# One task per weight split, and a seventh weight buffer in the feed forward of a two-layer decoder trunk

## The chip, the cores and the metric

The kernel runs on one NeuronCore of a Trainium2 chip. The metric is device time in microseconds, from the first to the last instruction with what the launch adds on the device. Before the change the median of three runs is 748.7 us (748.66 to 749.61).

## The reference

Two layers over 256 tokens of 1024 channels; each has a mixing part (dilated attention beside an mLSTM, with gates) and a feed forward. All of it is float32. The change concerns how the weights of all matmuls are brought in, and above all the feed forward:

```python
def hybrid_layer(x, ...):                      # DEPTH = 2
    h = rms_norm(x, norm_mix_w)
    z = h @ w_in + b_in                        # 1024 x 5640, columns go to q, k, v, gates ...
...
    yb = sigmoid(z[..., COL_MO:COL_MI]) * hm   # the mLSTM's output gate
    mixed = sigmoid(ga) * (ya @ w_proj_att) + sigmoid(gb) * (yb @ w_proj_mlstm)
    x = x + mixed @ w_out                      # 1024 x 1024
    h2 = rms_norm(x, norm_mlp_w)
    x = x + square(relu(h2 @ w_ff1)) @ w_ff2   # 1024 x 4096, 4096 x 1024
```

## The kernel before

**Weights.** Every matmul with weights is computed from float32r halves: a weight block w of 512 KB is split into hi, its rounded copy, and lo = w - hi, and TensorE multiplies hi by the activations' high and low part and lo by the high part. A *step* (class `Step`, line 237) is one such block with the 6 to 24 matmuls that use it. For each step SP loads the block into one of `N_RAW` = 6 buffers raw (line 385), ScalarE writes hi (`high`, one ACTIVATE), VectorE writes lo (`low`, one TENSOR_TENSOR), each into one of `N_SPLIT` = 5 buffers. Steps run on TensorE in the order of the list `steps`. A load waits until the block in its buffer has been split (`loads`, line 460); hi of step i waits for its block and for step i - 5 to be done (`highs`, line 495); lo waits for hi (`lows`, line 502). `highs` and `lows` are two tasks that go through all steps in order.

**Order.** Nothing in the program is ordered by hand. A scheduler (class `Scheduler`, line 299) runs at build time: tasks are generators that yield operations or flags that they need, a planner (`Plan`) keeps an estimated time for each engine and buffer, and the operation that can start soonest is written next into its engine's program; among those that start within about 0.1 us of it the lower rank wins. A split has rank 0.5 when TensorE needs it within 5 us by the plan, otherwise 4 (`slack`, line 472). On the chip each engine then runs its program strictly in order and waits on semaphores.

**Feed forward.** `w_ff1` makes eight hidden blocks of 512 channels. Blocks 0 to 5 (`BY_SEVEN`) are multiplied by `w_ff2` with seven products instead of eight (`by_seven`, line 1154); here they are called groups 0 to 5. A group has seven steps in this order: b11, t1, t3, b22, t2, b21, t4. Four have a weight load (b11, t3, b22, b21); t3's buffer first receives a block called b12. `weight_sums` (line 1138) builds the others: VectorE adds b11 + b12 into a total (t1; the totals are the tiles va and num in turn), a transfer issued by POOL then adds b22 to b12 in place (t3), another adds b22 to the total when lo of t1 is done (t2), and when lo of t2 is done VectorE adds b21 to the total (t4). So one total serves three steps, one after the other, and the buffers of b11 and b21 are only free when t1 and t4 are made. Between the groups' steps stand the `w_ff1` steps of the later hidden blocks, each block in two halves of two pieces; the first half of block 7 is called h7 below. At the end of a layer the order is: h7 (two pieces), group 4's t2, b21, t4, the second half of block 7 (two pieces), group 5's b11, t1, t3, b22, then two `w_ff2` steps of block 6, group 5's t2, b21, two more steps of block 6, group 5's t4, and four steps of block 7. The low half of a group's activations goes through a tile called zc for group after group, so that the next group's cast into zc waits until TensorE is done with t4.

**The gate's memory.** mog (line 395) has the shape of a raw buffer. It holds the mLSTM's output gate: `mog_evac` (line 808) fills it, `gates`, `output_gate` and `mlstm_out` (line 915) use it, and nothing touches it in the feed forward. The flags mix0 to mix3 are set when the four parts of `mixed` are there, at the end of the mixing part.

In the profile all operations have the line of a helper, L203, so rows are told apart by their tiles.

Of the kernel before, what the change touches and what calls it, by code (L numbers as in the profile page):

```python
# [298 lines left out]
class Scheduler:  # L299
# [8 lines left out]
    def add(self, gen, rank=3):  # L308
        self.tasks.append(Task(gen, rank))

    def mark(self, *flags):
        self.done.update(flags)
# [44 lines left out]
def trunk(ctx: ExitStack, tc: tile.TileContext, x_in, positions, norm_mix_w, w_in, b_in, conv_w, conv_b,  # L357
# [85 lines left out]


    steps, loaded = [], []
    at = {"step": 0, "part": 0.0}
    begins_at = [0.0]

    def new_step(src, view, dur, fn, raw=None, free=None):

        i = len(steps)
        load = len(loaded) if src is not None else None
        step = Step(i, raws[load % N_RAW] if raw is None else raw, load, src, view, dur, fn, free)
        if load is not None:
            loaded.append(step)
        steps.append(step)
        begins_at.append(begins_at[-1] + dur)
        return step

    def loads(first):  # L460
        for n in range(first, len(loaded)):
            yield Need(*loaded[n - N_RAW].free)
            yield load(n)
            mark(loaded[n].flag)

# [3 lines left out]
            return sync.dma_start(out=out, in_=src)  # L469
        return sync.dma_start(out=out[:, j, c], in_=src[:, j, c])  # L470

    def slack(i):

        def rank():
            k = i if isinstance(i, int) else at[i]
            now_at = begins_at[at["step"]] + at["part"] * steps[at["step"]].dur
            due = now["pe"] + begins_at[k] - now_at
            return 0.5 if due - now["act" if i == "hi" else "vec"] < 5.0 else 4
        return rank

    def high(i, j=slice(0, 2), c=slice(0, None)):
        st = steps[i]
# [9 lines left out]
            h, l, r = h[:, j, c], l[:, j, c], r[:, j, c]  # L492
        return vec.tensor_tensor(l, r, h, op=OP.subtract)

    def highs(first):
        for i in range(first, len(steps)):
            at["hi"] = i
            yield Need(("raw", i), ("step", i - N_SPLIT))
            yield high(i)
            mark(("hi", i))  # L500

    def lows(first):
        for i in range(first, len(steps)):
            at["lo"] = i
            yield Need(("hi", i))
            yield low(i)
            mark(("lo", i))


    KEEP = 2  # L510
# [248 lines left out]
    def layer(l, X, Y):  # L759
# [332 lines left out]
        def hid(f):  # L1092

            return tuple(s[:, 4 * (f % 2):4 * (f % 2) + 4, :] for s in X)
# [59 lines left out]
        def by_seven(f):  # L1154

            i = {}
            seven[f] = i
            last = f == BY_SEVEN[-1]

            def one(name, product, n, src=None, raw=None):  # L1160
                def fn(k, hi, lo):
                    yield Need(tag(f"q{f}"))
                    if product not in prods:
                        prods[product], = yield Take(banks)
                    o, new = prods[product], f == BY_SEVEN[0]
                    yield Need(("hi", k))
                    order = [(j, part) for j in range(2) for part in range(2)] + [(j, 2) for j in range(2)]
                    for at_, (j, part) in enumerate(order):
                        at["part"] = at_ / 6
                        if part == 2:  # L1170
                            yield Need(("lo", k))
                        yield mm(o[:], (shared.q_l, shared.q_h, shared.q_h)[part][:, n, j, :], (hi, hi, lo)[part][:, j, :],
                                 new and at_ == 0, last and at_ == 5 and product not in ("p2", "p3", "p4"))
                    if name == "t4":
                        mark(tag(f"seven{f}"))
                    if name == "t2" and last:
                        add(flush(), 1.5)
                step = new_step(src, wide(512), 1.395, fn, raw)
                i[name] = step.i
                return step  # L1180

            def w(kp, c):
                return rows(w_ff2[l], 4 * f + 2 * kp, 512 * c, 512)

            def total():
                return shared.total[f % 2]


            todo = (("b11", "P1", 0, w(0, 0), None), ("t1", "p5", 3, None, total), ("t3", "P7", 6, w(0, 1), None),
                    ("b22", "p3", 5, w(1, 1), None), ("t2", "P6", 4, None, total), ("b21", "p2", 1, w(1, 0), None),  # L1190
                    ("t4", "p4", 2, None, total))
            at_begin, made = len(steps) - 6, {}
            starts.append((at_begin, lambda: add(weight_sums(f, i, made), weight_rank)))

            def weight_rank():
                return slack(i["t1"])()

            for k, what in enumerate(todo):
                made[what[0]] = one(*what)
                if k in (1, 3, 5, 6):  # L1200

                    if k == 6:
                        made["b11"].free = [("lo", i["b11"]), ("raw", i["t1"])]
                        made["b21"].free = [("lo", i["b21"]), ("raw", i["t4"])]
                    if k == 3:
                        i["b12"] = ("b12", l, f)
                        made["t3"].flag = ("raw", i["b12"])
                    yield
# [160 lines left out]
        for c in range(2):  # L1369
            by_token(w_out[l], 512 * c, 512, X, (0, 1, 2, 3), out_evac(c), flags=lambda kp: [tag(f"mix{kp}")])  # L1370
        starts.append((len(steps), lambda: add(last_loads(), 3)))
        f0, f1 = {}, {}
        for kp in range(4):
            by_feature(w_ff1[l], 0, Y, (kp,), 0, 3, f0, ff_evac(0), flags=lambda kp: [tag(f"h{kp}")])
# [31 lines left out]
        if l + 1 < DEPTH:  # L1406
            for c in range(2):
                whole(7, c)
        else:
            by_token_last(w_ff2[l], lambda: hid(7), [out_norm(c) for c in range(2)], acc, 28, lambda kp: [tag(f"f7{kp}")])  # L1410

    starts = []
    X, Y = slot
# [75 lines left out]
    def first_split(n):  # L1489
        i, j, c, flags = pieces[n]  # L1490
        yield Need(f"piece{n}", ("xh", 0, 0), *[("hi", *p[:1], *f) for p in pieces[:n] for f in p[3]])
        yield high(i, j, c)
        mark(*[("hi", i, *f) for f in flags])
        yield low(i, j, c)
        mark(*[("lo", i, *f) for f in flags])
        if n + 1 == len(pieces):
            mark(("hi", 0), ("lo", 0), ("hi", 1), ("lo", 1))
            add(highs(2), slack("hi"))
            add(lows(2), slack("lo"))

    def first_x():
        yield from warm(WARM[0])
# [31 lines left out]
    def main():  # L1534
        begins = {}
        for i, fn in starts:
            begins.setdefault(i, []).append(fn)
        for i, st in enumerate(steps):
            if i in begins:
                for fn in begins[i]:  # L1540
                    fn()
            at["step"], at["part"] = i, 0.0
            yield from st.fn(i, st.view(his[i % N_SPLIT]), st.view(los[i % N_SPLIT]))
            mark(("step", i))

    at["hi"] = at["lo"] = 0
    mark(*[(kind, -i) for kind in ("step", "lo") for i in range(1, 10)])
    add(first_loads(), 0)
    add(first_params(), 2)
    add(first_constants(), 0)  # L1550
# [34 lines left out]
```

## Time and profile before

| | |
|---|---|
| median of three runs | 748.7 us (748.66 to 749.61) |
| the profiled execution | 749.45 us, of which its span is 747.6 |
| TensorE (PE) | busy 735.1 us, 98%; 5123 matmuls |
| weight loads on TensorE (PEld) | busy 674.9 us, 90% |
| VectorE (DVE) / ScalarE (ACT) / GpSimd (POOL) | busy 587.5 / 454.6 / 82.8 us |
| granted TensorE clock | 0.997 of full speed |
| DMA | 148.77 MB, mean 199 GB/s |

The span runs from the first to the last instruction. Matmuls overlap: each begins before the row of the one before it ends, so TensorE's pace is read from starts. Waits are put down to the semaphore that came last. SP's loads are issued by its queue (SPq); POOL's rows of DMA_DIRECT2D are the making of a transfer's descriptors, and its landing comes later.

### The profile page before, as it was taken

To read this page: it belongs to the slowest core of one execution; us is meant where nothing else is said; L and a number is where in the kernel's file an instruction comes from. 1 tells how busy PE (TensorE), PEld (TensorE's weight loads), DVE (VectorE), ACT (ScalarE), POOL (GpSimd) and SP (SyncE) were. 2 spreads that over 40 slices of the span, in tenths; PEclk is the share of its full clock that TensorE was granted. 3 is DMA by queue.
4 is the path that set the end of the run, shared out by engine and by line. 5 is a ranking of instruction groups with operands and counts; after the bars stand their busy time and mean duration, and the time that the engine had idled before them with its cause. 6 is when DMAs were issued, how large, how long until landed. Compare 5 with 4: busy or idle time off the path is not lost.

```text
span 747.6 us, 13242 instructions
## 1 busy us (share of the span) xinstructions
PE 735.1 (98%) x5123; PEld 674.9 (90%) x5123; DVE 587.5 (79%) x870; ACT 454.6 (61%) x708; POOL 82.8 (11%) x130
## 2 busy tenths in 40 slices
PE   9999999999999999999999999999999999999995
PEld 8989889998899999978899898899989999999774
DVE  5897887568658888977979988956776779887966
ACT  6657776545656577655656467845455756675752
POOL 4764010000010011100000000000000001101100
PEclk9999999999999999999999999999999999999998
DMA  9857553555567888877664654355555788888652
GB/s 310 294 183 222 169 164 120 191 187 181 171 196 224 239 238 235 246 198 226 234 217 130 212 179 146 115 172 194 174 190 173 181 250 216 260 253 233 190 165 85
DMA packets 90079, 148.77 MB, mean 199 GB/s; under 512 B 5176, under 2 KB 31712, under 8 KB 90016
## 3 DMA queue, kind: packets, MB, share of 16 engines
q1 hardware_dynamic: 82272, 133.63, 54.1%
q0 software_dynamic: 7440, 14.00, 10.7%
q8 instruction: 40, 0.66, 0.3%
q10 hardware_dynamic: 304, 0.30, 0.1%
q14 instruction: 23, 0.19, 0.1%
HBM read 146.32 MB, written 1.05 MB: 197 GB/s over the span
## 4 chain that ended last, share of the span: by engine, by line
PE 89%; issue 3%; DVE 3%; DMA 3%; ACT 1%; POOLq 0%; DVEq 0%; POOL 0%; ACTq 0%
PE bank L203 89%; DVE lo L203 2%; DMA raw<-in_w_ff 2%; DMA num<-in_w_ff 1%; ACT hi L203 1%; DVE x L203 0%; DVE big L203 0%; ACT slot0h L203 0%; DVE num L203 0%; DVE va L203 0%; DVE sg L203 0%; POOLq L1581 0%; POOL small L203 0%; DVEq L1581 0%; DVE small L203 0%
## 5 line engine op out<-in xcount | busy, mean ns | idle before, releaser
L203 DVE TENSOR_TENSOR lo<-raw,hi 128x1024 fp32r<-128x1024 f32 (+3 forms) x251 | 300.7, 1210 | 92.8 <-ACT hi L203 92.1
L203 ACT ACTIVATE hi<-raw 128x1024 fp32r<-128x1024 f32 (+3 forms) x251 | 259.6, 1045 | 147.4 <-PE bank L203 122.0
L203 PE MATMUL bank<-slot1l,hi 128*128 128x256 f32 x576 | 162.7, 283 | 0.0
L203 PE MATMUL bank<-slot1h,lo 128*128 128x256 f32 x576 | 162.3, 282 | 0.2 <-DVE lo L203 0.2
L203 PE MATMUL bank<-slot1h,hi 128*128 128x256 f32 x576 | 162.3, 282 | 0.0
L203 PE MATMUL bank<-slot0h,hi 128*128 128x256 f32 x576 | 161.5, 282 | 0.1
L203 PE MATMUL bank<-slot0h,lo 128*128 128x256 f32 x576 | 160.8, 283 | 0.3 <-DVE lo L203 0.3
L203 PE MATMUL bank<-slot0l,hi 128*128 128x256 f32 x576 | 160.9, 282 | 0.0
L203 PEld LDWEIGHTS bank<-slot0h,hi 128*128 128x128 f32 x576 | 107.9, 188 | 1.7 <-ACT hi L203 0.7
L203 PEld LDWEIGHTS bank<-slot1h,hi 128*128 128x128 f32 x576 | 108.3, 188 | 1.1 <-issue 0.5
L203 PEld LDWEIGHTS bank<-slot1l,hi 128*128 128x128 f32 x576 | 108.2, 188 | 1.2 <-issue 0.3
L203 PEld LDWEIGHTS bank<-slot1h,lo 128*128 128x128 f32 x576 | 108.4, 188 | 0.6 <-DVE lo L203 0.4
L203 PEld LDWEIGHTS bank<-slot0h,lo 128*128 128x128 f32 x576 | 107.5, 188 | 1.3 <-DVE lo L203 0.8
L203 PEld LDWEIGHTS bank<-slot0l,hi 128*128 128x128 f32 x576 | 107.8, 188 | 0.8 <-issue 0.2
L203 PE MATMUL bank<-hi,sg 128*128 128x512 f32 x168 | 66.5, 396 | 2.7 <-ACT hi L203 2.7
L203 PE MATMUL bank<-hi,zc 128*128 128x512 f32 x168 | 66.2, 394 | 0.0
L203 POOL DMA_DIRECT2D raw<-in_w_ff x12 | 14.5, 1210 | 365.0 <-DVE va L203 164.9
L203 PE MATMUL bank<-lo,zc 128*128 128x512 f32 x168 | 53.0, 396 | 0.2
L203 PE MATMUL bank<-hi,slot1h 128*128 128x512 f32 (+2 forms) x132 | 48.0, 364 | 0.0
L203 PE MATMUL bank<-lo,slot1h 128*128 128x512 f32 (+2 forms) x132 | 47.7, 361 | 0.0
L203 PE MATMUL bank<-hi,slot1l 128*128 128x512 f32 (+2 forms) x132 | 47.6, 361 | 0.0
L203 PE MATMUL bank<-hi,slot0h 128*128 128x512 f32 (+1 forms) x128 | 47.2, 369 | 0.0
(186 smaller groups left out, 1058.1 us busy)
## 6 DMA issues: line engine op xcount, KB each, us to landing
raw<-in_w_ff SPq DMA_DIRECT2D x128, 512.0 KB
raw<-in_w_in SPq DMA_DIRECT2D x78, 512.0 KB
raw<-in_w_out SPq DMA_DIRECT2D x16, 512.0 KB
raw<-in_w_ff POOLq DMA_DIRECT2D x12, 512.0 KB, 5.8
raw<-in_w_in SPq DMA_DIRECT2D x8, 520.0 KB
raw<-in_w_proj_mlstm SPq DMA_DIRECT2D x8, 512.0 KB
raw<-in_w_proj_att SPq DMA_DIRECT2D x8, 512.0 KB
va<-in_w_ff POOLq DMA_DIRECT2D x6, 512.0 KB, 7.7
```

The costliest lines, as they stand in the source:

```text
L203: f(*args, **kw)
```

## The change

Three things. Buffers come from a list, `ring`: a step with a load takes the buffer at its head, keeps the function that tells what frees it, and puts the buffer back at the end. Before the first feed-forward step of a layer mog is put at the head of the list, to be free when mix0 to mix3 are set, and after the last one it is taken out, so that the feed forward has seven buffers and the rest of the layer six. And `highs` and `lows` are gone: `split(i)` makes one task for each step, added when step i - 5 is done; it waits for its block alone, so a step whose block comes late no longer holds up the splits of the steps behind it in the plan.

```diff
+    ring = [(t, lambda: []) for t in raws]
...
-        step = Step(i, raws[load % N_RAW] if raw is None else raw, load, src, view, dur, fn, free)
         if load is not None:
+            raw, before = ring.pop(0)
+        step = Step(i, raw, load, src, view, dur, fn, free)
+        if load is not None:
+            step.before = before
+            ring.append((raw, lambda: step.free))
             loaded.append(step)
...
     def loads(first):
         for n in range(first, len(loaded)):
-            yield Need(*loaded[n - N_RAW].free)
+            yield Need(*loaded[n].before())
             yield load(n)
             mark(loaded[n].flag)
...
-    def highs(first):
-        for i in range(first, len(steps)):
-            at["hi"] = i
-            yield Need(("raw", i), ("step", i - N_SPLIT))
+    def split(i):
+
+        engine = ["act"]
+
+        def rank():
+            return slack(i, engine[0])
+
+        def parts_of():
+            yield Need(("raw", i))
             yield high(i)
             mark(("hi", i))
-
-    def lows(first):
-        for i in range(first, len(steps)):
-            at["lo"] = i
-            yield Need(("hi", i))
+            engine[0] = "vec"
             yield low(i)
             mark(("lo", i))
+
+        add(parts_of(), rank)
...
         starts.append((len(steps), lambda: add(last_loads(), 3)))
+
+        ring.insert(0, (mog, lambda: [tag(f"mix{k}") for k in range(4)]))
         f0, f1 = {}, {}
...
             by_token_last(w_ff2[l], lambda: hid(7), [out_norm(c) for c in range(2)], acc, 28, lambda kp: [tag(f"f7{kp}")])
+        ring[:] = [(t, free) for t, free in ring if t is not mog]
...
             mark(("step", i))
+            if i + N_SPLIT < len(steps):
+                split(i + N_SPLIT)
```

The change moves instructions at the end of each feed forward. On VectorE around group 4's t2 and t4 in layer 0, before (lo and hi are the split's buffers, raw the weight buffers, va and num the totals of groups 4 and 5, big an evacuated piece of block 7, slot0 the hidden activations):

```order
L203 TENSOR_TENSOR lo_106<-va_2045,hi_101 128x2x512
L203 TENSOR_TENSOR lo_107<-raw_96,hi_102 128x2x512
L203 TENSOR_TENSOR lo_108<-raw_97,hi_103 128x2x512
L203 TENSOR_TENSOR lo_104<-raw_98,hi_99 128x1024
L203 CAST slot0h<-big_75 128x512
L203 TENSOR_TENSOR lo_105<-raw_93,hi_100 128x1024
L203 TENSOR_TENSOR slot0l<-big_75,slot0h 128x512
L203 TENSOR_TENSOR num_2046<-raw_97,raw_98 128x1024
L203 TENSOR_TENSOR lo_106<-va_2045,hi_101 128x2x512
L203 TENSOR_TENSOR lo_107<-raw_94,hi_102 128x2x512
L203 TENSOR_TENSOR va_2045<-va_2045,raw_94 128x1024
L203 CAST slot0h<-big_76 128x512
```

and now:

```order
L203 TENSOR_TENSOR lo_106<-va_2042,hi_101 128x2x512
L203 TENSOR_TENSOR lo_108<-raw_96,hi_103 128x2x512
L203 TENSOR_TENSOR lo_107<-raw_95,hi_102 128x2x512
L203 TENSOR_TENSOR lo_104<-raw_97,hi_99 128x1024
L203 CAST slot0h<-big_75 128x512
L203 TENSOR_TENSOR lo_105<-raw_98,hi_100 128x1024
L203 TENSOR_TENSOR slot0l<-big_75,slot0h 128x512
L203 TENSOR_TENSOR lo_107<-mog,hi_102 128x2x512
L203 TENSOR_TENSOR num_2043<-raw_95,raw_96 128x1024
L203 TENSOR_TENSOR lo_106<-va_2042,hi_101 128x2x512
L203 TENSOR_TENSOR va_2042<-va_2042,mog 128x1024
L203 TENSOR_TENSOR lo_104<-raw_93,hi_99 128x1024
```

The first row is lo of t1 of group 4, followed by t3's and b22's (now b22's, then t3's), those of h7's two pieces, the sum into num for group 5, lo of t2 and the sum for t4 into va. The lo of b21 (from raw_94 before, from mog now) has moved ahead of the sum into num, and the cast of big_76 behind t4.

On SP, the loads from group 4's b22 on, with what each waits for (DVE is VectorE, Activation ScalarE, DMAHW and DMASW transfers), before:

```order
L203 DMA raw_97<-in_w_ff 128x2x512 [waits DMAHW2_49,DVE_49]
L203 DMA raw_98<-in_w_ff 128x4x256 [waits DMAHW3_49,DVE_49]
L203 DMA raw_93<-in_w_ff 128x4x256 [waits DMAHW4_49,DVE_49]
L203 DMA raw_94<-in_w_ff 128x2x512 [waits DMAHW5_49,DVE_49]
L203 DMA raw_95<-in_w_ff 128x4x256 [waits DMAHW6_49,DVE_49]
L203 DMA raw_96<-in_w_ff 128x4x256 [waits DMASW3_49,DVE_49]
L203 DMA raw_97<-in_w_ff 128x2x512 [waits DMAHW0_49,DVE_49]
L203 DMA raw_98<-in_w_ff 128x2x512 [waits DMAHW7_49,DMAHW1_49,DVE_49]
```

and now:

```order
L203 DMA raw_96<-in_w_ff 128x2x512 [waits DMAHW1_49,DVE_49]
L203 DMA raw_97<-in_w_ff 128x4x256 [waits DMAHW2_49,DVE_49]
L203 DMA raw_98<-in_w_ff 128x4x256 [waits DMAHW3_49,DVE_49,Activation_49]
L203 DMA mog<-in_w_ff 128x2x512 [waits DMAHW4_49,DVE_49]
L203 DMA raw_93<-in_w_ff 128x4x256 [waits DMAHW5_49,DVE_49]
L203 DMA raw_94<-in_w_ff 128x4x256 [waits DMAHW6_49,DVE_49]
L203 DMA raw_95<-in_w_ff 128x2x512 [waits DMASW3_49,DVE_49]
L203 DMA raw_96<-in_w_ff 128x2x512 [waits DMAHW7_49,DMAHW0_49]
```

The last two rows are group 5's b11 and b12. Their buffers held b22 and h7's first piece before, and hold t3 and b22 of group 4 now; the last row no longer waits for VectorE.

On VectorE around group 5's t2 in layer 0, before:

```order
L203 TENSOR_TENSOR lo_105<-raw_94,hi_100 128x2x512
L203 TENSOR_TENSOR lo_106<-raw_95,hi_101 128x2x512
L203 TENSOR_TENSOR slot0l<-big_77,slot0h 128x512
L203 TENSOR_TENSOR lo_107<-num_2046,hi_102 128x2x512
L203 TENSOR_TENSOR lo_108<-raw_96,hi_103 128x2x512
L203 TENSOR_TENSOR lo_104<-raw_97,hi_99 128x2x512
L203 TENSOR_TENSOR lo_105<-raw_98,hi_100 128x2x512
L203 TENSOR_TENSOR num_2046<-num_2046,raw_96 128x1024
```

and now:

```order
L203 TENSOR_TENSOR lo_105<-raw_98,hi_100 128x2x512
L203 TENSOR_TENSOR lo_106<-mog,hi_101 128x2x512
L203 TENSOR_TENSOR slot0l<-big_77,slot0h 128x512
L203 TENSOR_TENSOR lo_108<-raw_93,hi_103 128x2x512
L203 TENSOR_TENSOR lo_104<-raw_94,hi_99 128x2x512
L203 TENSOR_TENSOR lo_105<-raw_95,hi_100 128x2x512
L203 TENSOR_TENSOR lo_107<-num_2043,hi_102 128x2x512
L203 TENSOR_TENSOR num_2043<-num_2043,raw_93 128x1024
```

The lo of t2 (from num) has moved behind the three lo of b21 and of block 6's last two steps.

## Rows read from the trace of the kernel before

**Rows 1.** The page, part 1: busy time of each engine.
```profile
PE 735.1 (98%) x5123; PEld 674.9 (90%) x5123; DVE 587.5 (79%) x870; ACT 454.6 (61%) x708; POOL 82.8 (11%) x130
```
**Rows 2.** Busy time by stretches; columns as in the first line.
```profile
core 0: us, PE busy (x) PEld busy (x) DVE busy (x) ACT busy (x) POOL busy (x), PEclk, DMA share, GB/s
300.00:310.00 10.00, 10.00 (x68) 9.17 (x68) 9.39 (x11) 6.16 (x8) 1.18 (x1) 1.00 0.66 221
...
330.00:340.00 10.00, 8.54 (x53) 7.01 (x53) 9.90 (x11) 7.79 (x9) 0.34 (x1) 1.00 0.74 197
```
**Rows 3.** Timeline, TensorE, layer 0: start, length, out<-in, [idle before <-releaser].
```profile
328.26 0.28 PE L203 MATMUL bank<-slot1l,hi 128*128 128x256 f32 x1
...
328.85 0.39 PE L203 MATMUL bank<-hi,sg 128*128 128x512 f32 x1
...
329.54 0.40 PE L203 MATMUL bank<-hi,zc 128*128 128x512 f32 x1
...
331.31 0.63 PE L203 MATMUL bank<-lo,zc 128*128 128x512 f32 x2
333.17 0.50 PE L203 MATMUL bank<-hi,sg 128*128 128x512 f32 x1 [1.23 <-ACT hi L203]
...
335.79 0.28 PE L203 MATMUL bank<-slot1h,hi 128*128 128x256 f32 x1
```
**Rows 4.** Timeline, TensorE, layer 1, group 4's t4.
```profile
696.88 0.63 PE L203 MATMUL bank<-lo,zc 128*128 128x512 f32 x2
...
701.34 0.28 PE L203 MATMUL bank<-slot0h,hi 128*128 128x256 f32 x1
```
**Rows 5.** Timeline, TensorE, layer 1, group 5's t2.
```profile
717.56 0.39 PE L203 MATMUL bank<-lo,slot1h 128*128 128x512 f32 x1
...
719.47 0.73 PE L203 MATMUL bank<-lo,zc 128*128 128x512 f32 x2
```
**Rows 6.** The chain that ended last, layer 0: start, length, what.
```profile
320.61 6.69 DMA raw<-in_w_ff
```
**Rows 7.** Timeline, VectorE, layer 0, groups 4 and 5.
```profile
316.40 2.35 DVE L203 TENSOR_TENSOR lo<-raw,hi 128x1024 fp32r<-128x1024 f32 x2
...
327.39 1.23 DVE L203 TENSOR_TENSOR num<-raw,raw 128x1024 f32<-128x1024 f32 x1 [4.74 <-DMA raw<-in_w_ff]
328.53 1.22 DVE L203 TENSOR_TENSOR lo<-va,hi 128x1024 fp32r<-128x1024 f32 x1
```
**Rows 8.** Timeline, ScalarE, layer 0, the same place.
```profile
325.07 1.06 ACT L203 ACTIVATE hi<-va 128x1024 fp32r<-128x1024 f32 x1 [4.28 <-DMA va<-in_w_ff]
...
329.04 0.60 ACT L203 ACTIVATE big<-bank 128x512 f32<-128x512 f32 x1 [1.97 <-PE bank L203]
```
**Rows 9.** The chain that ended last, layer 1.
```profile
707.62 9.38 DMA num<-in_w_ff
```
**Rows 10.** Timeline, VectorE, layer 1, group 5's total num.
```profile
692.95 1.23 DVE L203 TENSOR_TENSOR num<-raw,raw 128x1024 f32<-128x1024 f32 x1 [4.56 <-DMA raw<-in_w_ff]
...
705.86 1.22 DVE L203 TENSOR_TENSOR lo<-num,hi 128x1024 fp32r<-128x1024 f32 x1
...
718.20 1.22 DVE L203 TENSOR_TENSOR lo<-num,hi 128x1024 fp32r<-128x1024 f32 x1 [5.98 <-ACT hi L203]
```
**Rows 11.** Timeline, ScalarE, layer 1, group 5's t2.
```profile
717.10 1.06 ACT L203 ACTIVATE hi<-num 128x1024 fp32r<-128x1024 f32 x1 [6.72 <-DMA num<-in_w_ff]
```
**Rows 12.** Timelines of ScalarE and TensorE, layer 0, group 3's t2.
```profile
300.84 1.06 ACT L203 ACTIVATE hi<-num 128x1024 fp32r<-128x1024 f32 x1 [1.27 <-DMA num<-in_w_ff]
...
307.67 0.39 PE L203 MATMUL bank<-hi,sg 128*128 128x512 f32 x1
```
**Rows 13.** Timelines of VectorE and TensorE, between the layers.
```profile
369.40 1.40 DVE L203 SCALAR_TENSOR_TENSOR x<-bank,small,x 128x512 f32<-128x512 f32 x2
...
372.32 0.60 PE L203 MATMUL bank<-ident,x 128*128 128x128 f32 x4
```
**Rows 14.** DMA issues: out<-in queue op xcount, KB each, median us to landing.
```profile
va<-in_w_ff POOLq DMA_DIRECT2D x6, 512.0 KB, 7.7
num<-in_w_ff POOLq DMA_DIRECT2D x6, 512.0 KB, 8.4
```

More of the change, by code (lines that the diff above doesn't have):

```diff
@@ L470, in load, with slack @@
         return sync.dma_start(out=out[:, j, c], in_=src[:, j, c])
[L472 to L479, printed above, removed]
+    def slack(i, engine):
+        now_at = begins_at[at["step"]] + at["part"] * steps[at["step"]].dur
+        return 0.5 if now["pe"] + begins_at[i] - now_at - now[engine] < 5.0 else 4
     def high(i, j=slice(0, 2), c=slice(0, None)):
@@ L1195, in weight_rank @@
             def weight_rank():
-                return slack(i["t1"])()
+                return slack(i["t1"], "vec")
             for k, what in enumerate(todo):
@@ L1497, in first_split @@
             mark(("hi", 0), ("lo", 0), ("hi", 1), ("lo", 1))
-            add(highs(2), slack("hi"))
-            add(lows(2), slack("lo"))
+            for k in range(2, N_SPLIT):
+                split(k)
     def first_x():
@@ L1544, in main @@
             mark(("step", i))
-    at["hi"] = at["lo"] = 0
-    mark(*[(kind, -i) for kind in ("step", "lo") for i in range(1, 10)])
+            if i + N_SPLIT < len(steps):
+                split(i + N_SPLIT)
     add(first_loads(), 0)
```

## The prediction

> **What bounds the kernel now.** Four views, in this order. First the page's busy times: TensorE is busy for 735.1 of 747.6 us [rows 1], so whatever is gained must come out of TensorE's waits. Second, busy time by stretches: the reader is to see that an ordinary 10 us of the feed forward has no idle TensorE (300 to 310 us), and that 330 to 340 us holds only 8.54 us of it, at the same granted clock of 1.00, the 2.4 GHz level [rows 2]. Between the first 20 and the last 20 us of the span only four stretches of 10 us stay under 9.9: this one and the three from 690 to 720 us, all at the end of a feed forward. Third, TensorE's own order of time at those places, because a matmul's row ends later than the next one starts and hides a part of a wait: there starts are to be compared. From 328.26 to 328.85 five matmuls of 256 columns start 0.118 us apart, from 328.85 to 329.54 three of 512 columns 0.23 us apart [rows 3]. From 331.31 to 335.79 there are eight of 512 and three of 256, which is 8 x 0.232 + 3 x 0.118 = 2.21 us, but 4.48 us pass: **2.27 us lost** in layer 0 [rows 3]. The same stretch in layer 1, 696.88 to 701.34, takes 4.46: **2.25 us lost** [rows 4]. From 717.56 to 719.47 five of 512 columns should take 1.16 and take 1.91: **0.75 us lost** [rows 5]. Together 5.3 us; that is all that waiting for split weights costs.
>
> Fourth, what TensorE waited for. In layer 0 it is t4 of group 4. Its chain goes back to a weight load of group 5: issued at 320.61, landed 6.69 us later [rows 6]. VectorE's program has the sum of group 5's t1 (num) ahead of the lo of group 4's t2, so VectorE sits idle for 4.74 us until that load lands; only at 328.53 come the lo of t2 and of b21, and then the sum that makes t4 [rows 7]. ScalarE had t2's hi ready at 325.07 + 1.06 = 326.13 [rows 8]. So a load that TensorE needs 15 us later holds up work that it needs at once. In layer 1 the 0.75 us have another cause: the adding transfer into num for t2 of group 5 lands 9.38 us after its issue, at 717.0, and ScalarE idles 6.72 us in front of t2's hi [rows 9, 11].
>
> **The change part by part.**
> - No instruction is added or removed: every engine keeps its count of rows, and TensorE's order differs only where x is transposed between the layers. So 0 us for work; all of it lies in waits.
> - The seventh buffer. A load now waits for the split of the load seven before it. Group 5's second load (b12) waited for the lo of h7's first piece, which ended just before 320.6. Now its buffer was freed by b22, and it stands right behind b11's load, which waits for t3's lo, the second of the pair that ends at 316.40 + 2.35 = 318.75 [rows 7]. With one issue of some 0.4 us between them it goes out at about 319.2, 1.4 us earlier; with the same 6.69 us [rows 6] it lands at 325.9 instead of 327.3. Bounds: not earlier at all (if the transfers share one bandwidth and end together), or 2.5 us earlier, since h7's last piece has been loaded before and is no longer in flight beside it. I take 1.4.
> - The split tasks. lo of b21 now stands ahead of that sum, and the cast and the subtraction of h7's output behind t4. From the sum on, at VectorE's 1.14 us from one such start to the next [rows 7]: sum 325.9 to 327.0, lo t2 to 328.2, the sum for t4 to 329.3, lo of the next step to 330.5. hi of t4 on ScalarE stands behind the evacuation that starts at 329.04 when TensorE has ended h7 [rows 8], so 329.6 to 330.7; lo of t4 to 331.9. TensorE gets to t4 at 331.31 + 2 x 0.23 = 331.8 and wants its lo four matmuls later, at 332.7. **Both 2.27 and 2.25 us go, with 0.8 us to spare.** What is late next is t4 itself again, by the evacuation, and it is in time.
> - Group 5's t2. Its adding transfer needs lo of t1, 705.86 + 1.14 = 707.0 [rows 10]. Between the sum at 692.95 and that lo there lies a cast into zc that must wait for TensorE's t4, so it comes at least the 2.25 us earlier that TensorE does; b21's lo and a subtraction, 1.14 and 0.6 us, have also left this stretch, so up to 3.3 us (one of them may have lain in the wait). The transfer lands 9.38 later [rows 9], at 713.7 to 714.7; t2's hi is done 1.06 later [rows 11], at 714.8 to 715.8, while TensorE now comes to t2 at 717.56 + 0.23 - 2.25 = 715.5. lo t2 has moved behind three other lo and ends at 716.1 to 716.9, wanted at 716.45. Left over: 0 to 0.5 us; I take 0.2, so **0.55 of the 0.75 us goes**.
> - SP and POOL. The first load into the output gate's memory stands ahead of the other feed-forward loads and waits for nothing in the built program, since its last reader is long done; nothing queues behind it. Before layer 1 writes the gate again, its last split lies more than ten steps back. Cost 0; if that cover were gone, one lo, 1.14 us.
>
> Sum: 2.27 + 2.25 + 0.55 = 5.1 us. The profiled execution took 749.45 us, its span of 747.6 and 1.85 around it, and is 0.75 above the median of the three runs, 748.7. Against its own time the sum gives 744.35, against the median **743.6 us**.
>
> **The rivals.**
> 1. The load lands no earlier (327.3). For: loads of 512 KB pile up there, 6.69 us each [rows 6]. Against: the same bytes start sooner. Then t2's lo ends at 329.7, t4's hi at 331.95, its lo at 333.1: 0.2 and 0.2 us late, so 0.5 us stays in each layer and 0.4 of group 5: 5.1 - 1.0 - 0.4 = 3.7 us of gain, 745.0.
> 2. The adding transfers get longer because one more load is in flight beside them, and the wait for them takes the place of the one removed; this one ends slower. They take 7.7 and 8.4 us in the median and 9.38 at the longest [rows 14, 9]. By the Trainium skill, "DMA: Bandwidth & Descriptors", section "Issuing engines are not separate DMA queues", transfers from the SP and POOL queues run on the same 16 engines and interleave, which speaks against this change; with that page's 436 GB/s another 512 KB is 1.2 us, an estimate. In the rows: groups 0 to 3 have room (group 3's t2 has its hi done at 301.90 for a matmul at 307.67, 5.8 us [rows 12]); group 4 has 0.9 us before the order above shifts (326.13 to 327.0) and 0.8 us to spare at t4, group 5 none. A lateness d costs 2(d - 1.7) + 2d = 4d - 3.4 us over both layers. At the rows' own spread of 1.7 us (7.7 to 9.38) that is 3.4 us, 747.0; from d = 2.1 the gain is gone, and from 2.5 the kernel is slower by over 0.2%; at 3.5 it is 754.2. Against: group 4's transfer had four loads issued during its flight before, and has four now.
> 3. Between the layers VectorE now has one more lo ahead of the two sums into x that finish half of x, and TensorE's first transposition of x stands eight matmuls, 1.86 us, earlier. In the trace these sums end at 370.8, and the transposition starts at 372.32 [rows 13]; moved, it comes at 370.5. If VectorE is as late as before plus 1.14, TensorE waits 1.5 us: 745.1; if that lo has to wait as long as the sum above did, 4.74 us more, 749.8. Against: three lo have moved into VectorE's idle time before group 5's t2, 5.98 us long in layer 1 [rows 10], so VectorE should come to x ahead of TensorE.
>
> **How the numbers follow.** The forecast (waits gone but for a remainder) has 0.65, rival 1 0.17, rival 2 0.09, rival 3 0.09. The gain cannot pass the 5.3 us lost, 743.4; the low end, 742.5, leaves 0.9 us for the median of a few runs, the spread of the three shown (748.66 to 749.61). The high end, 746.5, takes in rivals 1 and 3 at their usual price and most of the way to rival 2's 747.0; beyond it lie some 0.12. About 0.2%, 1.5 us, is what a measurement of this kernel can tell from no change: faster means below 747.2. The forecast, rival 1, most of rival 3 and a part of rival 2 lie there: 0.90. Within it, rival 2 near d = 2.1 and rival 3 at its worst: 0.06. Slower: rival 2 beyond d = 2.5: 0.04.
>
> **What would show it.** In the changed profile: no gap before t4 of group 4 in either layer, so that 330 to 340 and 690 to 700 us read 10.00; VectorE's wait for a weight load ahead of num shrinks from 4.74 to about 3 us without TensorE feeling it; t2 of group 5 in layer 1 starts within 0.5 us of the matmul before it; TensorE's busy time stays near 735 us while its last matmul comes 5 us earlier. Wrong would be: a gap of more than 0.5 us at t4 that still ends on VectorE's lo (rival 1), adding transfers of 10 us and more (rival 2), or a new gap at the transpositions of x near 365 us (rival 3).

## The result, and the profile after

The changed kernel takes **742.8 us** (median of four runs, 742.50 to 743.34) against 749.1 us (748.66 to 749.61) of the kernel before: a ratio of **0.9917, 95% interval 0.9900 to 0.9934**, or 6.2 us less (4.9 to 7.5). Forecast were 743.6 us, a gain of 5.1 on 748.7; a fourth execution has moved the median of before to 749.1, which is 0.4 of the difference between the two gains. The interval holds 5.1, so that more was gained than forecast is read from the traces: the profiled execution took 742.73 us with a span of 740.9, 6.7 us less than the profiled one of before.

The page, part 1, after: TensorE's busy time falls by 2.5 us only [rows 1], though the same 5123 matmuls run. The rows of matmuls that wait are longer, so busy time held a part of the waits.

```profile
PE 732.6 (99%) x5123; PEld 675.4 (91%) x5123; DVE 588.0 (79%) x870; ACT 456.3 (62%) x708; POOL 82.5 (11%) x130
```

Busy time by stretches, the end of layer 1 before, then both layers after: the columns are those of [rows 2]. 330 to 340 us holds 10.00 us of TensorE where it held 8.54, and the three stretches at the end of layer 1 are full too (8.72, 9.82 and 9.68 before), at the same granted clock of 1.00.

```profile
690.00:700.00 10.00, 8.72 (x57) 7.25 (x56) 6.96 (x8) 5.63 (x7) 1.20 (x1) 1.00 0.71 203
700.00:710.00 10.00, 9.82 (x65) 8.93 (x66) 10.00 (x10) 8.25 (x11) 1.20 (x1) 1.00 0.68 213
710.00:720.00 10.00, 9.68 (x41) 7.24 (x40) 4.02 (x5) 3.28 (x5) 0.00 (x0) 1.00 0.88 255
```

```profile
330.00:340.00 10.00, 10.00 (x68) 9.20 (x67) 10.00 (x11) 8.12 (x10) 0.86 (x1) 1.00 0.87 260
...
690.00:700.00 10.00, 10.00 (x69) 9.02 (x68) 9.97 (x11) 7.57 (x10) 1.20 (x1) 1.00 0.79 222
700.00:710.00 10.00, 10.00 (x54) 8.47 (x53) 9.93 (x10) 5.96 (x8) 1.20 (x1) 1.00 0.80 200
710.00:720.00 10.00, 10.00 (x45) 8.07 (x44) 8.61 (x10) 7.61 (x9) 0.00 (x0) 1.00 0.37 142
```

The timelines of SP, VectorE, ScalarE and TensorE in layer 0, after (start, length, what; the places of [rows 3, 7, 8]). SP issues the two loads of group 5 one right after the other: together they end at 319.88, so the second, 0.65 long, goes out at 319.23. VectorE has the lo of b21 (from mog) ahead of the sum into num, waits 2.49 us for the load instead of 4.74, and has t4's lo at 331.04, by 332.26. TensorE's eight matmuls of 512 and three of 256 columns from 331.15 to 333.37 take 2.22 us, their pace.

```profile
318.77 1.11 SPq L203 DMA_DIRECT2D raw<-in_w_ff  x2
...
322.57 1.23 DVE L203 TENSOR_TENSOR lo<-mog,hi 128x1024 fp32r<-128x1024 f32 x1
326.29 1.23 DVE L203 TENSOR_TENSOR num<-raw,raw 128x1024 f32<-128x1024 f32 x1 [2.49 <-DMA raw<-in_w_ff]
327.43 1.22 DVE L203 TENSOR_TENSOR lo<-va,hi 128x1024 fp32r<-128x1024 f32 x1
...
331.04 1.22 DVE L203 TENSOR_TENSOR lo<-va,hi 128x1024 fp32r<-128x1024 f32 x1
...
329.94 1.06 ACT L203 ACTIVATE hi<-va 128x1024 fp32r<-128x1024 f32 x1 [0.31 <-DVE va L203]
...
331.15 0.62 PE L203 MATMUL bank<-lo,zc 128*128 128x512 f32 x2
331.61 0.39 PE L203 MATMUL bank<-hi,sg 128*128 128x512 f32 x1
...
332.55 0.63 PE L203 MATMUL bank<-lo,zc 128*128 128x512 f32 x2
...
333.37 0.28 PE L203 MATMUL bank<-slot1h,hi 128*128 128x256 f32 x1
```

The same in layer 1: at t4 a wait of 0.1 us is left (the last pair of lo matmuls takes 0.73 us instead of 0.63), and at group 5's t2 five matmuls of 512 columns from 712.78 to 713.94 take 1.16 us where they took 1.91 [rows 5].

```profile
695.62 0.73 PE L203 MATMUL bank<-lo,zc 128*128 128x512 f32 x2
...
700.70 1.22 DVE L203 TENSOR_TENSOR lo<-num,hi 128x1024 fp32r<-128x1024 f32 x1
...
711.28 1.06 ACT L203 ACTIVATE hi<-num 128x1024 fp32r<-128x1024 f32 x1
...
712.78 0.39 PE L203 MATMUL bank<-lo,slot1h 128*128 128x512 f32 x1
713.00 0.39 PE L203 MATMUL bank<-hi,sg 128*128 128x512 f32 x1
...
713.94 0.63 PE L203 MATMUL bank<-lo,zc 128*128 128x512 f32 x2
```

The DMA issues, after: the adding transfers into the totals (t2) have become shorter, 7.7 to 5.8 and 8.4 to 7.6 us in the median [rows 14], those into a raw buffer (t3) longer: 5.8 before, 7.4 and 7.5 now.

```profile
raw<-in_w_ff POOLq DMA_DIRECT2D x10, 512.0 KB, 7.4
va<-in_w_ff POOLq DMA_DIRECT2D x6, 512.0 KB, 5.8
num<-in_w_ff POOLq DMA_DIRECT2D x6, 512.0 KB, 7.6
mog<-in_w_ff POOLq DMA_DIRECT2D x2, 512.0 KB, 7.5
```

The end of the program, first before, then after: TensorE's last matmul, and VectorE's last sum into x, which needs it.

```profile
739.43 0.28 PE L203 MATMUL bank<-lo,slot1h 128*128 128x256 f32 x1
...
740.82 0.48 DVE L203 SCALAR_TENSOR_TENSOR x<-bank,small,x 128x256 f32<-128x256 f32 x1
```

```profile
733.81 0.28 PE L203 MATMUL bank<-lo,slot1h 128*128 128x256 f32 x1
...
734.12 0.48 DVE L203 SCALAR_TENSOR_TENSOR x<-bank,small,x 128x256 f32<-128x256 f32 x1
```

Before, the last matmul ended at 739.71 and VectorE came to its sum 1.1 us later; now the matmul ends at 734.08 and the sum starts at 734.12: VectorE is on time. From the start of that sum to the end of the span, stores included, it is 6.8 us in both. The chain that ended last (start, length, what) fits that, first before, then after. Before, it left TensorE for good at 721.60, 18 us ahead of the last matmul, and went through VectorE's lo, its sums for t4 and into x to the end. After, it is one piece of TensorE from 64.10 to 728.48 us, 4631 matmuls in which the chain shows no wait (the 0.1 us at t4 in layer 1 is too short for it); it leaves there by a sum into x that had waited for TensorE, so that VectorE is on time at the very end is read from the two rows above.

```profile
719.47 2.13 PE bank L203 x8
...
721.61 1.22 DVE lo L203
...
734.77 1.41 DVE x L203 x2
```

```profile
64.10 664.38 PE bank L203 x4631
...
728.51 0.76 DVE x L203
```

So the 6.7 us between the two spans are **5.6 us that TensorE's last matmul comes earlier** and **1.1 us of VectorE's arrears at the very end**.

Where TensorE's 5.6 us lie comes from its starts: over all matmuls, the time from one start to the next less the pace of its width (0.118 us for 256 columns, 0.232 for 512), summed. Before, 2.53 us are lost from 320 to 360 us and 3.12 from 690 to 730; after, 0.12 and 0.13. Across the transpositions of x between the layers 0.2 us more is gained: ahead of them the same matmul comes 2.44 us earlier than before, behind them 2.68.

### The profile page after: what moved, and what is told of

Same layout as the page of the kernel before. It is cut to its first block, busy times and chain, and to the rows that moved or that the text cites. A ratio compares the mean times of both kernels' runs of the same rounds, so it can differ in the third digit from the quotient of the medians.

```text
span 740.9 us, 13202 instructions
## 1 busy us (share of the span) xinstructions
PE 732.6 (99%) x5123; PEld 675.4 (91%) x5123; DVE 588.0 (79%) x870; ACT 456.3 (62%) x708; POOL 82.5 (11%) x130
## 3 DMA queue, kind: packets, MB, share of 16 engines
HBM read 146.32 MB, written 1.05 MB: 199 GB/s over the span
## 4 chain that ended last, share of the span: by engine, by line
PE 98%; issue 1%; ACT 0%; DVE 0%; POOLq 0%; POOL 0%; DVEq 0%; ACTq 0%
PE bank L203 98%; ACT slot0h L203 0%; ACT hi L203 0%; DVE lo L203 0%; DVE x L203 0%; ACT big L203 0%; POOLq L1589 0%; POOL small L203 0%; DVEq L1589 0%; DVE sg L203 0%; DVE ones L203 0%; DVE small L203 0%; POOLq L203 0%; ACTq L203 0%
## 5 line engine op out<-in xcount | busy, mean ns | idle before, releaser
L203 DVE TENSOR_TENSOR lo<-raw,hi 128x1024 fp32r<-128x1024 f32 (+3 forms) x231 | 277.8, 1209 | 91.4 <-ACT hi L203 90.3
L203 ACT ACTIVATE hi<-raw 128x1024 fp32r<-128x1024 f32 (+3 forms) x231 | 240.3, 1046 | 169.8 <-PE bank L203 144.3
L203 POOL DMA_DIRECT2D raw<-in_w_ff x10 | 12.2, 1215 | 323.4 <-DVE va L203 163.8
```

Of the source, the lines that this page charges most:

```text
L203: f(*args, **kw)
```

## The experiments

The experiments ran on three chips, each time beside the kernel before, which has a median of 750.2 to 750.5 us there; ratios are to it. By 11 us into the span TensorE is up to 2.3 us behind the profile of before, differently in each execution, so the same place can stand 2 us later in another profile. The table has, for each kernel, what TensorE loses by its starts at the end of each layer's feed forward (320 to 360 and 690 to 730 us), how far VectorE's last sum into x comes behind the last matmul, the gain that follows from these three against before (2.53 + 3.12 + 1.1 less what is left), and the gain by the ratio with its interval.

| kernel | layer 0 | layer 1 | VectorE behind | gain by trace | gain measured, us |
|---|---|---|---|---|---|
| before | 2.53 | 3.12 | 1.1 | | |
| the change | 0.12 | 0.13 | 0.0 | 6.5 | 6.2 (4.9 to 7.5) |
| the change, again | 0.11 | 0.02 | 0.0 | 6.6 | 7.3 (5.9 to 8.6) |
| split tasks alone | 1.02 | 1.05 | 0.0 | 4.7 | 4.2 (3.2 to 5.1) |
| seventh buffer alone | 2.52 | 2.73 | 1.1 | 0.4 | 1.2 (0.4 to 2.0) |
| before, sum later | 0.67 | 0.59 | 0.0 | 5.5 | 4.8 (3.8 to 5.9) |
| split tasks, sum later | 0.69 | 0.62 | 0.0 | 5.4 | 5.3 (4.1 to 6.5) |
| before, a load held | 2.52 | 2.43 | 0.0 | 1.8 | 2.8 (1.9 to 3.7) |
| the change, a load held | 0.81 | 0.03 | 0.0 | 5.9 | 6.8 (5.5 to 8.0) |
| the change, held and later | 0.71 | 0.62 | 0.0 | 5.4 | 5.4 (4.1 to 6.8) |

**1. Split tasks alone.** The change without its seventh buffer:

```diff
-        ring.insert(0, (mog, lambda: [tag(f"mix{k}") for k in range(4)]))
...
-        ring[:] = [(t, free) for t, free in ring if t is not mog]
```

> The changed kernel without the gate's memory in the ring: six raw buffers, one task per split. Theory A (the order of VectorE's program carries the gain, the earlier load only gives it the room): group 5's second load goes out at 320.6 us as before and lands at 327.3, so the sum into num stands at 327.4 instead of 326.3, and everything behind it on VectorE is 1.1 us later than in the changed kernel. There the lo of group 4's t4 was ready 0.29 us (layer 0) and 0.05 us (layer 1) ahead of its matmul: 0.8 and 1.05 us are lost, the rest of the gain stays, the last matmul to the end of the span takes 6.8 us as in the changed kernel. 742.8 + 1.9 = 744.7 us. The adding transfer into va for group 4's t2 takes 7.9 us again, because a load goes out 0.6 us behind its issue (5.6 in the changed kernel, where none does). Rival B (the earlier load carries the gain, the order nothing): 749.1 us. Rival C (the seventh buffer gives nothing): 742.8 us.

Ratio 0.9944 (0.9932 to 0.9957). The sum into num stands at 327.42 as computed, t4's lo 1.1 us later than in the change, and 0.8 us is lost at t4 in each layer, in layer 1 another 0.2 ahead of it, at t2's lo: theory A. Two things in the expectation were wrong: the adding transfer for group 4's t2 takes 5.9 us and not 7.9, because the split order has moved the load behind it to 1.76 us after its issue (experiment 5 takes this up); and the span ends 7.7 us after the last matmul, although VectorE is on time, for the last store lands 0.9 us later in this execution.

```profile
327.42 1.23 DVE L203 TENSOR_TENSOR num<-raw,raw 128x1024 f32<-128x1024 f32 x1 [3.52 <-DMA raw<-in_w_ff]
...
332.16 1.23 DVE L203 TENSOR_TENSOR lo<-va,hi 128x1024 fp32r<-128x1024 f32 x1
...
332.19 0.50 PE L203 MATMUL bank<-hi,sg 128*128 128x512 f32 x1 [0.23 <-ACT hi L203]
```

**2. The seventh buffer alone.** The kernel before with these parts of the change:

```diff
+    ring = [(t, lambda: []) for t in raws]
...
+            raw, before = ring.pop(0)
...
+        ring.insert(0, (mog, lambda: [tag(f"mix{k}") for k in range(4)]))
```

> The kernel before with the ring and the gate's memory as seventh buffer, and the splits still two tasks that go through all steps in order. Theory A: group 5's second load lands 1.1 us earlier, at 326.2, and VectorE's order is that of before, so the sum, lo of t2, lo of b21 and the sum for t4 all come 1.1 us earlier; the wait for t4 of group 4 falls from 2.27 to 0.6 to 1.2 us in each layer, group 5's t2 in layer 1 still waits some 0.75, and the last matmul to the end of the span still takes 7.9 us. Gain 2.2 to 3.3 us: 746.3 us (745.8 to 746.9). Rival B (the earlier load carries all): 743.6 us or less. Rival C (it gives nothing without the order): 749.1 us.

Ratio 0.9984 (0.9973 to 0.9995): a fifth of the gain, less than theory A gave it. TensorE is 1.75 us behind the profile of before from its first microseconds on in this execution; with that taken off, SP issues group 5's second load at 318.8 instead of 320.61, 1.8 us earlier, but the sum stands at 326.57 instead of 327.39, only 0.8 earlier: the load takes 7.7 us. And the adding transfers are longer, 8.6 and 8.7 us for group 4's t2 (7.9 before) and 9.4 for group 5's in both layers (8.6 and 9.4 before). So TensorE still loses 1.6 us around group 4's t4 in layer 0, and now 0.8 at group 5's t2 there, where it lost nothing: the second rival of the prediction, in one profile. Group 5's 9.4 us can also be chance, since before has 8.6 in one layer and 9.4 in the other with loads at the same distances.

```profile
319.40 1.50 SPq L203 DMA_DIRECT2D raw<-in_w_ff  x2
...
328.32 1.23 DVE L203 TENSOR_TENSOR num<-raw,raw 128x1024 f32<-128x1024 f32 x1 [3.92 <-DMA raw<-in_w_ff]
...
352.49 1.06 ACT L203 ACTIVATE hi<-num 128x1024 fp32r<-128x1024 f32 x1 [6.69 <-DMA num<-in_w_ff]
...
353.60 0.50 PE L203 MATMUL bank<-hi,sg 128*128 128x512 f32 x1 [0.21 <-ACT hi L203]
```

**3. The sum out of the way.** The kernel before, with one more flag that group 5's sum into num needs when the order is planned:

```diff
-            yield Need(("raw", i["b11"]), ("raw", i["b12"]), tag("hidden"), *([("lo", seven[f - 2]["t4"])] if f > 1 else []))
+            yield Need(("raw", i["b11"]), ("raw", i["b12"]), tag("hidden"), *([("lo", seven[f - 2]["t4"])] if f > 1 else []),
+                       *([("lo", seven[f - 1]["t2"])] if f == 5 else []))
```

> The kernel before with one more thing that group 5's sum into num waits for: the lo of group 4's t2, so that VectorE's program has lo of t2, lo of b21 and the sum for t4 ahead of it. No buffer, no split task and no load is changed, and TensorE's order is that of before. Theory A (a sum that waits for a load stood ahead of work that was ready): hi of t2 is ready at 326.1, so lo of t2 ends at 327.3, the sum for t4 at 329.6, the sum into num at 330.7, lo of t4 at 332.3 where 332.7 is wanted: both waits at t4, 2.27 and 2.25 us, go. Group 5's t2 in layer 1 keeps a wait of 0.2 to 1.5 us, and the tail of 7.9 us stays. 749.1 - 4.5 = 744.6 us (743.9 to 745.6). Rival B (the weights come too late whatever the order): the sum, 2.2 us later at 330.7, hands its delay to group 5's first steps, and the time is 747 us or more.

Ratio 0.9936 (0.9922 to 0.9949), 4.8 us, with six buffers and the old split tasks: the waits at t4 are gone. VectorE now waits for t2's hi and not for the load, and then runs without a pause; when it comes to the sum, the load has landed. With TensorE's later start taken off, t2's lo and the sum for t4 come 2.2 us earlier than before, and up to there the sum into num is all that has moved. Behind it the new plan moves two more operations on VectorE in each layer. One is the subtraction of a piece of block 7's output (0.7 us), which stood ahead of t4's lo and now comes 8 us behind it; t4's lo is done 0.06 us before TensorE wants it, so by these rows some 0.7 us would still be lost at t4 without this move; no run leaves it in its place. What is left is 0.6 us per layer at the step behind t4, whose lo comes late. Group 5's t2 kept no wait, other than expected: its adding transfer takes 5.8 us instead of 9.4 (the next load goes out 2.1 us behind its issue instead of 0.66), and VectorE is on time at the end. So of the 5.5 us that the trace accounts for, 3.5 lie around t4 and 2.0 behind this transfer, which experiment 5 takes up.

```profile
327.05 1.23 DVE L203 TENSOR_TENSOR lo<-va,hi 128x1024 fp32r<-128x1024 f32 x1 [3.63 <-ACT hi L203]
...
330.46 1.22 DVE L203 TENSOR_TENSOR num<-raw,raw 128x1024 f32<-128x1024 f32 x1
...
332.06 1.22 DVE L203 TENSOR_TENSOR lo<-va,hi 128x1024 fp32r<-128x1024 f32 x1
...
334.48 0.39 PE L203 MATMUL bank<-slot1h,lo 128*128 128x256 f32 x1 [0.16 <-DVE lo L203]
```

**4. Split tasks, six buffers, the sum later.** Experiments 1 and 3 in one kernel.

> One task per split, six buffers, and group 5's sum into num behind the lo of group 4's t2: the changed kernel without its seventh buffer, with the sum put out of the way instead. Theory A (the seventh buffer matters only because the sum waits for its load): no wait is left at t4 of group 4 although the load lands as late as before, lo of t4 ends at 331.9 for 332.7, and the time is that of the changed kernel, 742.8 us (742.3 to 743.6), with a tail of 6.8 us. Rival (the earlier load helps by itself): 744 us or more, with a wait at group 5's steps.

Ratio 0.9929 (0.9914 to 0.9945). As theory A has it, no wait is left at t4 although the load lands as late as before (0.7 us to spare). But a new one of 0.6 us stands at group 5's t3 in each layer: its buffer can only receive b22 once the sum has read b12 there, and both its adding transfer (7.7 us) and its split come late. So the rival is partly right: by the trace the earlier load is worth those 1.2 us, because it lets the sum stand where it is early enough for group 5 and still not late for group 4. The ratio alone does not tell this kernel from the change, and the plan moves more than the sum here too (one cast of block 7's output goes from VectorE to ScalarE, another the other way).

```profile
340.00:350.00 10.00, 9.75 (x47) 7.66 (x46) 9.43 (x11) 7.15 (x9) 1.18 (x1) 1.00 0.81 200
...
345.15 0.73 PE L203 MATMUL bank<-lo,zc 128*128 128x512 f32 x2 [0.25 <-DVE lo L203]
```

**5. A load held back behind the adding transfer.** The kernel before, where two loads behind group 5's adding transfer exchange their buffers (the ring is used without mog):

```diff
+            raw, before = ring.pop(load in swapped)
...
                 i[name] = step.i
+                if last and name == "t3":
+                    swapped.add(step.load + 6)
```

> The kernel before, in which two loads behind group 5's adding transfer into num change buffers: the one that goes out 0.66 us behind the transfer's issue takes the buffer that the next split frees, and goes out 1.76 us behind it, the next one right after. Nothing else is moved; the order on every engine is that of before. Theory A (a load issued within some 1.2 us behind an adding transfer, while POOL still makes its descriptors for 1.18 us, lengthens it by about 2 us; one issued later does not): the transfer takes 5.6 to 6.5 us instead of 9.38 in layer 1 and 8.56 in layer 0. Then hi of group 5's t2 comes about 3 us earlier in layer 1, the 0.75 us that TensorE lost there go, VectorE does its backlog earlier, and the last matmul to the end of the span falls from 7.9 to 6.8 us: 1.85 us of gain, a ratio of 0.9975. Both waits at group 4's t4, 2.27 and 2.25 us, stay. Rival B (the transfer's time comes from all that moves during its flight, which is the same four loads): it stays at 8 us or more and the time is that of before.

Ratio 0.9963 (0.9951 to 0.9975), 2.8 us (1.9 to 3.7), where the trace accounts for 1.8; the other 1.0 is not explained. The first row is of the kernel before, the others of this one: the load behind the transfer into num goes out 0.65 us behind its issue there (708.27 after 707.62) and 1.76 us here.

```profile
708.27 0.37 SPq L203 DMA_DIRECT2D raw<-in_w_ff  x1
```

```profile
708.09 1.20 POOL L203 DMA_DIRECT2D num<-in_w_ff  x1 [11.70 <-ACT big L203]
...
709.85 0.37 SPq L203 DMA_DIRECT2D raw<-in_w_ff  x1
...
714.16 1.06 ACT L203 ACTIVATE hi<-num 128x1024 fp32r<-128x1024 f32 x1 [3.29 <-DMA num<-in_w_ff]
```

The transfer takes 6.0 us instead of 9.4 (5.7 instead of 8.6 in layer 0). TensorE's 0.75 us at group 5's t2 are gone, VectorE is on time at the end, and both waits at t4 stay: theory A, except that two distances do not show where its limit lies, nor that POOL's 1.2 us is it. That also shows where VectorE's arrears came from: 5.98 us of idle time in front of t2's lo [rows 10], with everything for the end of the layer queued behind it. In the change they go another way. Its transfer still takes 8.8 us, but VectorE does three lo in that time and idles only 1.33 us in front of the last of them; with the split tasks alone (8.5 us) the arrears are gone too, with the buffer alone they stay.

**6. The change with the same exchange.** As experiment 5, in the changed kernel.

> The changed kernel with the same exchange of two loads' buffers behind group 5's adding transfer. Theory A: the transfer falls from 8.5 (layer 0) and 8.8 us (layer 1) to 5.6 to 6.5, and the hi and lo of group 5's t2, 0.3 us ahead of their matmuls in the changed kernel, come 2 to 3 us ahead. As TensorE does not wait there in the changed kernel, the time stays: a ratio of 0.992, 742.8 us. Rival B (TensorE still loses something behind these transfers that the starts of its matmuls do not show): faster than the changed kernel by 0.5 us or more.

Ratio 0.9910 (0.9893 to 0.9927): no more than the change. The transfer falls to 5.8 and 5.7 us, but t2's lo still comes 0.3 us ahead of its matmul, since it stands behind three other lo in VectorE's program; the expected 2 to 3 us of room did not come. And in this execution the load of group 5 in layer 0 took 7.8 us, not 7.0, the sum stands 0.8 us later against TensorE, and 0.7 us is lost at t4.

```profile
329.31 1.23 DVE L203 TENSOR_TENSOR num<-raw,raw 128x1024 f32<-128x1024 f32 x1 [3.30 <-DMA raw<-in_w_ff]
...
334.09 0.50 PE L203 MATMUL bank<-hi,sg 128*128 128x512 f32 x1
...
335.35 0.74 PE L203 MATMUL bank<-lo,zc 128*128 128x512 f32 x2
```

**7. The change once more.**

> The changed kernel once more, unaltered, on the chip of the next run. Theory A (group 5's second load lands 7.0 to 7.8 us after its issue from one execution to the next, and the lo of group 4's t4 has 0.05 to 0.4 us to spare): ratio 0.9905 to 0.993, and in the profiled execution each of the two stretches at t4 loses between 0 and 0.8 us, as the load in it lands. Rival (the margin is the same in every execution): both stretches lose 0.1 us or less again.

Ratio 0.9903 (0.9886 to 0.9921). Nothing is lost at t4, and its lo has 0.66 and 0.54 us to spare, against 0.29 and 0.05 in the first profile: group 5's second load takes 6.6 us here in both layers, against 7.0 and 7.1. So the margin is not the same in every execution, but it and the load lie outside what theory A expected, and that both stretches lose 0.1 us or less again is what the rival said; this run by itself decides between neither. With experiment 6 the margin goes from -0.7 to +0.7 us, and the load from 7.8 to 6.6.

**8. The change with the exchange and the sum later.** The edits of 3 and 5 in the changed kernel.

> The changed kernel with the two loads behind group 5's adding transfer exchanged and, besides, group 5's sum into num behind the lo of group 4's t2, so that t4 no longer depends on when the load lands. Theory A: no wait is left at t4 and t2, and the time is 742.3 to 742.9 us, a ratio of 0.991 to 0.992: no better than the changed kernel by what a measurement can tell, only with 0.7 us or more to spare at t4. Rival B: the later sum makes group 5's t3 late, as in the kernel with six buffers, where 0.6 us were lost there in each layer: 743.5 to 744.0 us, 0.9925 to 0.993.

Ratio 0.9928 (0.9909 to 0.9946): rival B. t4 has 0.7 us to spare in both layers, and 0.6 us is lost at group 5's t3 in each. The exchange holds nothing back here: with the sum later, the next load goes out 0.63 us behind group 5's adding transfer all the same, and the transfer takes 7.8 us. No version beats the change by what these runs can tell.

```profile
340.00:350.00 10.00, 9.75 (x42) 7.41 (x42) 9.01 (x10) 7.31 (x8) 0.08 (x1) 1.00 0.92 261
...
700.00:710.00 10.00, 9.75 (x53) 7.97 (x52) 9.46 (x12) 6.91 (x8) 1.20 (x1) 1.00 0.82 214
```

## Why the prediction was right, and where it was off

**The waits at group 4's t4** (2.27 and 2.25 us): both are gone, as forecast, but for 0.1 us in layer 1. The cause, a sum that waits for a load ahead of ready work in VectorE's program, is shown by experiment 3: up to the sum for t4 it moves that sum alone, and this comes 2.2 us earlier. For the lo of t4 the moved subtraction has a share, there and in the change.

**The seventh buffer.** Its load goes out at 319.23 (forecast 319.2) and takes 7.0 us, not 6.69, so the sum stands at 326.29 and not 325.9. With lo of t4 done at 332.26 for a matmul at 332.55, 0.3 us are to spare where 0.8 were forecast. Rival 1, the load that lands no earlier, is the price without the buffer: 1.8 us more are lost over both layers in experiment 1, where the prediction had 1.0 at t4. And it is not far off in the change itself: in experiment 6, whose order is the change's at this place, 0.7 us of it came.

**The split tasks.** That t4's hi would wait for the evacuation of a bank was wrong: the row at 329.94 waits for VectorE's sum into va. hi starts at 329.94 and not 329.6, which is part of the 0.5 us by which the margin came out smaller.

**Group 5's t2**: 0.55 of 0.75 us forecast, all 0.75 came. The terms held: against a layer 0 that ends 2.64 us earlier, lo of t1 starts 2.5 us earlier in layer 1 (forecast 2.25 to 3.3), and hi of t2 is done 0.66 us before TensorE wants it. The transfer took 8.8 and not 9.38 us.

**Rival 2**, longer adding transfers, got a chance of 0.09, with a lengthening d that would be the same wherever one more load is in flight. That reading of the mechanism failed. In the change the transfer for group 4's t2 is 2.3 us shorter, and group 5's, where the prediction gave no room at all, is 0.1 and 0.6 us shorter. For these transfers it counts when the next load goes out, and the swapped lo of t3 and b22 had moved that for group 4. With the buffer alone the rival is there, and by that profile takes back most of what the buffer gives.

**Rival 3**: the transpositions of x come at 367.80, 4.5 us earlier, of which 2.4 are TensorE's own gain in layer 0 and 2.1 nine matmuls (the prediction counted eight, 1.86). No wait stands there; 0.2 us of before went as well.

**The step that failed is the first**: "whatever is gained must come out of TensorE's waits". It bounds the gain by 5.3 us, and 1.1 us came from outside: VectorE was 1.1 us late behind the last matmul. The chain of before had it, since it leaves TensorE at 721.60: the prediction read busy times and TensorE's starts, and of the chain only the pieces around the loads. It even had the cure, three lo that move into VectorE's idle time of 5.98 us, but used it for x between the layers alone and not for the end of the program. The bound was also too low for TensorE itself, whose last matmul comes 5.6 us earlier: its starts before lose 2.53 and 3.12 us, 5.65 together and not 5.3, since short waits, as at 329.81 and behind 719.47, were left out, and 0.2 us went at x. So the sum of 5.1 lacks 1.1 us at the end, 0.2 at group 5's t2, 0.2 at x and the short waits; 0.25 us of waits are left, and that gives the 6.7.

That 742.8 lies in the range is in part luck. By the prediction's own bound 743.4 was the least, and the low end, 742.5, was lowered for the spread of the runs, not for this.

## What to carry to other kernels

When an engine's busy share is 98%, look first for what its feeders do in program order: an operation that waits for a late transfer, ahead of one that is ready, holds up all that stands behind it (here 4.74 us of VectorE's time, of which 2.27 reached TensorE). One more flag for that operation (two lines) brought 4.8 us where the change brings 6.2, a part of it by what the new plan moved besides, so compare the order of every engine after such an edit. A further buffer pays where the order lets the earlier data be used; alone it brought 1.2 us, and some transfers were longer. At the end of a program ask which engine is in arrears when the busiest one stops: its delay is part of the time too.

## What the runs showed of the hardware

At some places an adding transfer's time goes with when the next load is issued behind it; POOL makes the transfer's descriptors for 1.17 to 1.20 us from its issue there. The ten profiles have 100 such transfers of 512 KB at five places (t3 of groups 2 to 4, t2 of groups 4 and 5, in both layers). Where the next load goes out 0.6 to 0.9 us behind the transfer's issue, 56 of them take 7.3 to 9.7 us; where it goes out 1.7 us or more behind, 44 take 5.6 to 6.2. The two do not overlap, and experiment 5 shows it for group 5's t2 by moving one load. At t3 of group 0 the step lies closer: 6.8 to 7.5 us with the next load 1.2 us behind, 5.7 to 6.4 with it 1.4 us behind (there a load ahead of the transfer has moved too, from 1.7 to 1.4 us).

It is not the only thing. t2 of groups 2 and 3, with two loads 1.4 and 2.5 us ahead of it, takes 7.3 to 9.0 us with no load close behind. t3 of group 1 takes 6.6 to 7.8 us in the five profiles with the seventh buffer, where loads go out 1.7 and 3.3 us ahead of it and the next one 3.9 us behind, and 5.6 to 6.2 in the other five. t3 of group 5 takes 6.8 to 7.7 us in experiments 4 and 8, where two loads go out within 3.6 us ahead of it, and 5.6 to 6.4 elsewhere. These places differ in the loads ahead of the transfer; no run here moves one of those alone, so that they are the cause is not shown, and why any of it is so stays open.

The Trainium skill, "DMA: Bandwidth & Descriptors", section "Issuing engines are not separate DMA queues", says that transfers of all issuing engines run on the same 16 DMA engines and interleave. The 56 transfers agree with that. By that rule alone a load issued 1.7 us behind should interleave as well and lengthen the transfer, and the 44, at 5.6 to 6.2 us, do not show it: t2 of group 0, whose next load goes out 6.1 us behind, takes 5.6 to 6.3.

Group 5's second load, a plain one of 512 KB, took 6.5 to 7.8 us from issue to landing in the seven profiles in which the sum waits for it, and 6.6 to 7.8 in the three of the change's order (landing taken as 0.09 us ahead of the sum, as in the kernel before); a margin of 0.3 us behind such a load is none.
